# A two-layer trunk on one core: three adaLN vectors computed on TensorE, x loaded in two transfers, and a new order of the first part

## The chip, the cores and the metric

The kernel runs on 1 core of one Trainium2 chip. The metric is device time in microseconds of that core; several runs are given by their median.

## The reference

The input x has 512 tokens of 1024 channels, in float32. Two layers follow one another, and both get shift, scale and gate vectors from one conditioning vector c:

```python
c_act = jax.nn.silu(c)
for i in range(DEPTH):                        # DEPTH = 2
    mods = c_act @ w_ada[i] + b_ada[i]        # 6 vectors of 1024
    sh1, sc1, g1, sh2, sc2, g2 = split(mods, 6)
    h = rms_norm(x, norm1_g[i]) * (1 + sc1) + sh1
    mix = s5_mixer(h, ...) if i == 0 else short_conv_mixer(h, ...)
    x = x + g1 * mix
    h = rms_norm(x, norm2_g[i]) * (1 + sc2) + sh2
    x = x + g2 * swiglu(h, w_ffn_in[i], w_ffn_out[i])     # hidden size 2816
return rms_norm(x, final_g)
```

The S5 mixer runs a diagonal complex state space over 64 groups of 16 channels (64 states per group, discretised from a, b, c and a log step), then GELU and an output projection to 2048 columns whose halves are multiplied as value times sigmoid(gate) (the GLU).

## The kernel before, in words

The vectors of a layer are numbered m = 0 to 5 in the order shift 1, scale 1, gate 1, shift 2, scale 2, gate 2; (0, 2) is gate 1 of the first layer, (0, 4) and (0, 3) are scale and shift of its FFN.

The residual lives transposed in SBUF (`xT`, channels on partitions, 512 tokens along the free axis). Every large product is three products of float32r parts: `acc3` multiplies high by high, high by low and low by high. `Weights` streams weight blocks of 128x4x256 through three raw buffers (`wr`, 512 KB each, SP's queue, L158); ScalarE copies the high part `wh`, VectorE or GpSimd subtracts for the low part `wl`.

The first part (class `Ssm`, up to the GELU) is a set of coroutines: loads, constants, discretisation (`params`), matrices of a chunk of 8 tokens (`vb`, `vm`, `w1m`, `w3m`), a scan over 64 chunks (`sup`, `sdn`), outputs (`yi`, `ye`, `yt`). Their order is a table written out by hand, `ORDER`: a name stands for one step of that coroutine, `*n` for n steps, and a letter behind the name for the engine that does its copies (V is VectorE, A ScalarE, G GpSimd). Each engine issues in the order of the table, so a step that is moved there moves on every engine and queue that it uses. `pre` and `wprep` in the table are the first GLU products and the split of their weights.

SP's queue begins with `loads`: a (`nat`, L785 and L786), x in four transfers (`xtok`, L796), b (`xT` used as a scratch place, L799), and then the 16 blocks `aw` for shift and scale of the first norm (`aload`, L835). On x the first squares are taken by ScalarE (`squares`, L1097); on b the transposes `bps` and the discretised matrices depend.

The adaLN vectors come in two ways. Shift and scale of the first norm (`gemv`, `gvec`) are row products on TensorE: a column of c, broadcast to 32 weights, against 256 columns of w_ada, into one of four quadrants of 32 output rows (`gmv`), four products in a step. All the other ten vectors go through class `Ada`: a partition holds 32 input channels of 256 columns (`ada`, four transfers of 256 KB at a time), VectorE multiplies the first channel (L226) and multiplies and adds the other 31 (`aacc`, through the helper at L122), and two small products on TensorE with `nsel` (`adaps`) add up the partitions. `Ada.step(n)` does the next n channels. For the first three vectors these steps stand in ORDER (`adas`, with `adal` for the loads) or between the two last GLU halves; the rest stands in the two FFNs.

L124 is the helper of all matrix products, L125 of transposes, L116 of two-operand VectorE or GpSimd steps, L122 of the multiply-and-add, L123 of steps with scalars, L126 and L127 of copies on ScalarE and VectorE. In the page's names `o<-yT,wh` are GLU products, `yps` the products of the mixer's outputs, `sr` the chunk states that they read, `ssq` the sum of squares for the second norm, and `mod` an adaLN vector. The dense work after the GLU (FFN, convolution mixer, FFN, final norm) is in plain program order.

Of the kernel before, what the change touches and what calls it, by code (L numbers as in the profile page):

```python
# [34 lines left out]
loads aload squares.0*2 aload squares.0*2 aload consts aload*5 c_load aload params squares.1 params squares.1
aload squares.1 aload squares.1 aload params aload params*5 zero params zero params*10 zero params*69 b_in
cm44*2 b_in cm44 b_in cm44 b_in cm44 b_in cm44 b_in stats b_in*2 stats b_in*2 cm44 stats gemv.0 stats trans
stats*2 trans gemv.0 vb.0 trans vb.0 trans vm.0.0.2 vecs stats vecs gemv.0 stats vm.0.1.0.V gemv.0*2 trans vb.1
gemv.0 vb.1 vm.0.0.2 vm.1.1.3.G*3 aload*2 trans gemv.0 trans gemv.0 stats*2 vm.0.1.1.G trans vecs stats gvec.0
stats vm.0.1.3.V aload stats vm.0.1.3.V vm.0.1.1.G hrows.0.0 vm.0.1.1.G hrows.0.0 vm.0.1.3.V vm.0.1.0.V  # L40
vm.0.1.2.G hrows.0.0 vm.0.1.2.G hrows.1.0 vm.0.1.2.G hrows.0.0 gvec.0 c_in*4 gvec.0*2 vm.0.0.1 gvec.0
vm.0.0.0.G*2 hrows.0.1*2 vm.0.0.0.G gvec.0 vm.0.1.0.V hrows.0.1 gemv.1 hrows.0.1 vm.0.0.2 w1m.0.1.0*2 gemv.1
vm.0.0.1 rp.A.V gvec.0 rp.A.V w1m.0.1.2.V rp.A.V*3 gemv.1 rp.A.V*2 c_blocks rp.A.V vm.0.0.1 rp.A.V vm.0.0.3
rp.A.V w1m.0.1.2.V vm.0.0.3 rp.A.V vm.1.1.0.G rp.A.V w1m.0.0.0.V vm.1.1.0.G w1m.0.1.1.V vm.0.0.3 c_blocks
rows_t.0.0 gemv.1 rows_t.0.0 vm.1.1.0.G w1m.0.0.0.V w1m.0.1.1.V vm.1.1.2.G*3 w1m.0.0.3.V rows_t.0.1 gemv.1
rows_t.0.1 hrows.1.0 gemv.1 umod.0.0.VAVAVAVAVVVAVAVA*2 w3m.0.0.1*2 umod.0.0.VAVAVAVAVVVAVAVA w3m.0.0.1 gemv.1
w1m.0.0.3.V w1m.0.0.1.A umod.0.0.VAVAVAVAVVVAVAVA gemv.1 sm.0.0.A*2 umod.0.1.VAVAVAVAVAVAVVVV w1m.0.0.1.A
c_blocks dkm umod.0.1.VAVAVAVAVAVAVVVV sm.0.1.A w3m.0.1.1 umod.0.1.VAVAVAVAVAVAVVVV hrows.1.0 sm.0.0.A c_blocks
umod.0.1.VAVAVAVAVAVAVVVV sm.0.1.A vm.1.0.0.V*2 gvec.1*3 vm.1.0.0.V sm.0.1.A hrows.1.0 krev.0 w1m.0.0.2.A*2
w3m.0.1.1 w1m.0.1.3.A hrows.1.1 sup.0.0*4 hrows.1.1 sup.0.0 krev.0*2 sup.0.0*4 sm.0.2.A hrows.1.1 w3m.0.1.1  # L50
w1m.0.1.3.A sup.0.0*2 krev.0 kfin.0.S*4 w3m.0.0.0 kfin.0.S sup.0.0 gvec.1 w3m.0.0.0 sm.0.2.A w3m.0.0.0 sup.0.0
vm.1.0.3 sm.0.3.A vm.1.1.1.G vm.1.0.3*2 vm.1.1.1.G*2 sm.0.2.A w1m.1.1.2.A*2 sup.0.0 sm.0.3.A gvec.1 sm.0.3.A
kfin.0.S w1m.1.1.0.A sup.0.0 sup.0.1 sup.0.0 hrows.1.1 rows_t.1.0 sup.0.0 vm.1.0.2.G sup.0.0 kfin.0.S
w1m.1.1.3.A sup.0.1 sup.0.0 sup.0.1 rows_t.1.0 w1m.1.1.0.A sup.0.0*3 gvec.1 kfin.0.S*4 rows_t.1.1 sup.0.1
vm.1.0.2.G gvec.1 sup.0.1 sup.0.0 vm.1.0.2.G rows_t.1.1 w1m.1.1.3.A umod.1.0.VAVAAAVVAAAAVAAV sup.0.1 yi.0.2
sup.0.0 umod.1.0.VAVAAAVVAAAAVAAV*2 yi.0.2 sup.0.0*3 umod.1.1.VVAAAAVVVAVAVAAA w3m.0.1.0 sup.0.1 sup.0.0
w3m.0.1.0 umod.1.1.VVAAAAVVVAVAVAAA umod.1.0.VAVAAAVVAAAAVAAV w3m.0.1.0 sup.0.0 sup.0.1 sup.0.0
umod.1.1.VVAAAAVVVAVAVAAA*2 sup.0.1 vm.1.0.1.V*3 w3m.1.0.0 sdn.0.0 krev.1*2 w3m.1.0.0 krev.1*2 sup.0.1
w1m.1.1.1.A*2 sdn.0.0 sup.0.1 sdn.0.0 sup.0.1 sdn.0.0 w1m.1.0.3.A sup.0.1 wprep.0 sdn.0.0*2 adal sup.0.1*2
sdn.0.0 sup.0.1 w3m.1.0.0 w1m.1.0.1.A*2 sdn.0.0 w1m.1.0.0.A sup.0.1*2 sdn.0.0 sm.1.1.A w1m.1.0.3.A sm.1.1.A  # L60
sdn.0.0*2 yi.0.1 yi.0.0 w1m.1.0.2.A sup.0.1 wprep.0 sup.0.1*6 sm.1.1.A sup.0.1 w1m.1.0.0.A sdn.0.0 sw.0.0.AAAA
sup.0.1 yi.0.0 sw.0.0.AAAA sm.1.3.A sw.0.0.AAAA w3m.1.1.1*3 yi.0.1 sup.0.1 sw.0.0.AAAA ye.0.0*3 sup.0.1 ye.0.0
sm.1.3.A wprep.0 w1m.1.0.2.A sm.1.2.A yi.0.3 sm.1.3.A yi.0.3 ye.0.0 sm.1.2.A wprep.1 w3m.1.1.0 ye.0.0 w3m.1.1.0
adal sup.0.1 sdn.0.1*12 sw.0.1.VAAA*4 sm.1.0.A*3 w3m.1.1.0 adas.0*2 adal sm.1.2.A adas.0*3 ye.0.1 adas.0 adal
ye.0.1*2 x_t.0.0.A sup.1.0.G x_t.0.0.A*2 x_t.1.1.A ye.0.1*2 x_t.1.1.A sup.1.0.G*3 adal sup.1.1.P sup.1.0.G*3
x_t.1.0.A adas.0 kfin.1.B sup.1.0.G wprep.1 ye.0.1 sup.1.0.G x_t.0.0.A x_t.1.1.A sup.1.1.P yt.0.0*2 x_t.1.0.A
yt.0.0*4 kfin.1.B*2 sup.1.1.P yt.0.1 wprep.1 yt.0.1*3 x_t.1.1.A yt.0.1*2 sup.1.1.P*2 kfin.1.B sup.1.1.P*2 adas.0
sup.1.1.P*2 pre.0 wprep.2.G sup.1.1.P*3 wprep.2.G sup.1.1.P wprep.2.G sup.1.1.P sup.1.0.G kfin.1.B sup.1.0.G*3
wprep.3 kfin.1.B sup.1.0.G*3 x_t.1.0.A kfin.1.B*2 pre.0 kfin.1.B*2 sup.1.0.G*2 pre.0 sup.1.0.G kfin.1.B adas.0
# [1391 lines left out]
```

## Time and profile before

| what | value |
|---|---|
| median of 3 runs | 1192.04 us (1191.62 to 1195.54) |
| profiled execution | span 1196.1 us from its first to its last instruction; the page gives no other time for it |
| TensorE busy | 1104.6 us (92%), mean granted clock 0.968 |
| VectorE busy | 725.4 us (61%) |
| ScalarE busy | 389.7 us (33%) |
| GpSimd busy | 195.4 us (16%) |
| moved by DMA | 153.48 MB |

The page cuts the span in 40 slices of about 30 us. TensorE's row has 9 in nearly every slice from the tenth on, and lower digits in the first nine, while VectorE's row has its 8 and 9 in the first six slices. So the dense part is TensorE's, and the first 275 us have to be read by stages. A row of waits names the waiting engine and line, what released it, and then the total in us, the number of waits and the longest one. A row of the timeline gives start and duration, and in brackets the idle time before.

### The profile page before, as it was taken

Reading aid. Unit: us, or ns where it says so; the run is one execution under the profiler, and the core shown is the slowest. Engines: PE = TensorE matmul, PEld = TensorE weight load, DVE = VectorE, ACT = ScalarE, POOL = GpSimd, SP = SyncE. Lnnn points to the kernel's source line nnn. Section 1 sums busy time; section 2 is a strip of 40 time slices with the busy share of each in tenths; the row PEclk is TensorE's granted clock in tenths of the full one; section 3 lists DMA queues with packets and bytes.
Section 4 is the critical chain, followed back from the end, with each engine's and each line's share of the span. In section 5 each row is a group of like instructions: output and inputs, shape, how many; then the busy total and the mean of one; then the engine's idle time right before and its main releaser. Section 6 shows DMA issues by size and latency. Waiting matters only on the chain.

```text
span 1196.1 us, 15760 instructions
## 1 busy us (share of the span) xinstructions
PE 1104.6 (92%) x6146; PEld 932.3 (78%) x6146; DVE 725.4 (61%) x1334; ACT 389.7 (33%) x628; POOL 195.4 (16%) x141
## 2 busy tenths in 40 slices
...
GB/s 237 155 64 154 163 149 225 137 71 71 195 200 186 88 171 174 195 129 107 180 102 88 206 161 137 148 106 72 106 106 106 90 86 106 102 94 88 77 27 71
DMA packets 150107, 153.48 MB, mean 128 GB/s; under 512 B 8864, under 2 KB 144140, under 8 KB 150032
## 3 DMA queue, kind: packets, MB, share of 16 engines
...
q0 software_dynamic: 288, 0.10, 0.1%
...
HBM read 147.99 MB, written 2.10 MB: 125 GB/s over the span
## 4 chain that ended last, share of the span: by engine, by line
PE 76%; DVE 15%; DMA 3%; issue 2%; ACT 2%; POOL 2%; SPq 1%; DVEq 0%; ACTq 0%; POOLq 0%
PE o L124 71%; DVE aacc L122 4%; PE t L124 2%; DMA ada<-in_w_ada_dram 1%; DMA xT<-in_ssm_b_re_dram 1%; DVE sg L116 1%; DVE xT L122 1%; DVE sx L116 1%; DVE hlo L122 1%; POOL sx L116 1%; DMA wr<-in_ssm_w_out_dram 1%; DVE acc L116 1%; DVE v L116 1%; DVE wl L116 1%; DVE u L123 1%
## 5 line engine op out<-in xcount | busy, mean ns | idle before, releaser
L124 PE MATMUL o<-wide,wh 128*128 128x512 f32 (+1 forms) x992 | 364.5, 370 | 1.8 <-ACT wide L469 1.8
L124 PE MATMUL o<-wide,wl 128*128 128x512 f32 (+1 forms) x992 | 363.7, 369 | 0.0
L124 PE MATMUL o<-hlo,wh 128*128 128x512 f32 (+1 forms) x992 | 354.7, 370 | 2.3 <-DVE hlo L122 2.2
L126 ACT ACTIVATE wh<-wr 128x1024 fp32r<-128x1024 f32 (+1 forms) x184 | 188.5, 1039 | 416.9 <-PE o L124 294.0
L116 DVE TENSOR_TENSOR wl<-wr,wh 128x1024 fp32r<-128x1024 f32 (+1 forms) x155 | 185.0, 1204 | 156.9 <-ACT wh L126 155.1
L124 PEld LDWEIGHTS o<-wide,wh 128*128 128x128 f32 x992 | 187.9, 189 | 33.4 <-ACT wide L469 2.6
L124 PEld LDWEIGHTS o<-wide,wl 128*128 128x128 f32 x992 | 187.8, 189 | 30.9
L124 PEld LDWEIGHTS o<-hlo,wh 128*128 128x128 f32 x992 | 182.8, 189 | 34.7 <-DVE hlo L122 3.1
L124 PE MATMUL o<-hid,wh 128*128 128x512 f32 (+1 forms) x704 | 205.4, 375 | 0.0
L122 DVE SCALAR_TENSOR_TENSOR aacc<-ada,cper,aacc 128x256 f32<-128x256 f32 x310 | 187.4, 605 | 29.0 <-DMA ada<-in_w_ada_dram 20.5
L116 POOL TENSOR_TENSOR wl<-wr,wh 128x1024 fp32r<-128x1024 f32 x29 | 71.4, 2473 | 595.8 <-ACT wh L126 579.5
L124 PEld LDWEIGHTS o<-hid,wh 128*128 128x128 f32 x704 | 129.2, 188 | 23.7
L124 PE MATMUL o<-hid,wl 128*128 128x512 f32 (+1 forms) x352 | 131.8, 375 | 0.0
L116 DVE TENSOR_TENSOR sg<-sg,o 128x512 f32<-128x512 f32 (+1 forms) x50 | 31.7, 644 | 154.3 <-PE o L124 152.3
L124 PE MATMUL o<-yT,wh 128*128 128x512 f32 (+1 forms) x256 | 77.4, 383 | 13.8 <-DVE yT L116 10.1
L525 ACT ACTIVATE sg<-o 128x512 f32<-128x512 f32 (+1 forms) x48 | 26.8, 562 | 170.4 <-PE o L124 168.8
L124 PEld LDWEIGHTS o<-hid,wl 128*128 128x128 f32 x352 | 66.3, 188 | 11.9
L122 DVE SCALAR_TENSOR_TENSOR xT<-o,mod,xT 128x512 f32<-128x512 f32 (+1 forms) x56 | 38.8, 693 | 57.4 <-PE o L124 57.2
L124 PEld LDWEIGHTS o<-yT,wh 128*128 128x128 f32 x256 | 48.5, 198 | 23.4 <-issue 7.7
L124 PE MATMUL o<-yT,wl 128*128 128x512 f32 (+1 forms) x128 | 48.7, 380 | 0.0
L439 ACT ACTIVATE sq<-xT 128x256 f32<-128x256 f32 (+1 forms) x44 | 20.7, 472 | 62.9 <-DVE xT L122 57.3
L124 PE MATMUL o<-z,wh 128*128 128x512 f32 (+1 forms) x128 | 33.1, 348 | 4.6 <-ACT z L126 4.6
...
## 6 DMA issues: line engine op xcount, KB each, us to landing
wr<-in_w_ffn_in_dram SPq DMA_DIRECT2D x88, 512.0 KB, 3.6
...
wr<-in_w_ffn_out_dram SPq DMA_DIRECT2D x40, 512.0 KB, 4.4
wr<-in_conv_w_in_dram SPq DMA_DIRECT2D x24, 512.0 KB, 3.8
aw<-in_w_ada_dram SPq DMA_DIRECT2D x16, 512.0 KB, 10.2
wr<-in_ssm_w_out_dram SPq DMA_DIRECT2D x16, 512.0 KB, 9.1
wr<-in_conv_w_out_dram SPq DMA_DIRECT2D x8, 512.0 KB, 7.6
xtok<-in_x_dram SPq DMA_DIRECT2D x4, 512.0 KB, 8.2
```

The source lines that it names most:

```text
L116: (eng or e.V).tensor_tensor(out=out, in0=a, in1=b, op=op)
L122: e.stt = lambda o, a, s, b, op0, op1: e.V.scalar_tensor_tensor(out=o, in0=a, scalar=s, in1=b, op0=op0, op1=op1)
L123: e.ts = lambda o, a, s1, s2, op0, op1: e.V.tensor_scalar(out=o, in0=a, scalar1=s1, scalar2=s2, op0=op0, op1=op1)
L124: e.mm = lambda o, l, r, start, stop: e.PE.matmul(out=o, lhsT=l, rhs=r, start=start, stop=stop)
L126: e.cp = lambda o, i: e.A.activation(out=o, in_=i, func=AF.Copy)
L439: A.activation(out=q, in_=xT[:, k, SL[s]], func=AF.Square)
L525: A.activation(out=w, in_=g[:, 0:width(s)], func=AF.Silu)
```

## The change

It has four pieces.

1. (0, 2), (0, 4) and (0, 3) leave `Ada`, whose list now starts with (0, 5); `adal`, `adas` and the two `ada.step` calls of the GLU go. `gload` loads the columns of the three vectors as 12 blocks of 1 MB, and `gemm(m)` makes each vector by 32 row products on TensorE in four steps of eight, a copy by ScalarE, four small products with a new constant `sel2`, and an addition (for m = 4 a second VectorE step).
2. x comes in two transfers of 1 MB to 128 partitions instead of four of 512 KB to 64.
3. ORDER is a new table, with other steps side by side and other engines for some copies.
4. Comments are gone, so lines move by a few: the matrix helper is L120, two-operand steps are L112.

The diff, without comments and with one line of the table before and after:

```diff
+GEMV = (2, 4, 3)
 ORDER = """
-sup.1.0.G*3 pre.1 sup.1.0.G sup.1.1.P pre.1*6 sup.1.1.P adas.0 yi.1.0 sup.1.0.G sdn.1.1.G*5 sdn.1.0*5 yi.1.0
+sup.1.0.G sup.1.1.P gemm.4 sup.1.1.P pre.1*3 x_t.0.1 pre.1*2 yi.1.0 sup.1.0.G gemm.4 sup.1.0.G*7 sdn.1.0*4 yi.1.0
...
-    ada = e.ada = Ada(e, [(0, 2), (0, 4), (0, 3), (0, 5), (1, 1), (1, 0), (1, 2), (1, 4), (1, 3), (1, 5)])
+    ada = e.ada = Ada(e, [(0, 5), (1, 1), (1, 0), (1, 2), (1, 4), (1, 3), (1, 5)])
...
-        def adal():
-            for _ in range(8):
-                ada.load()
-                yield
-
-        def adas(v):
-            for _ in range(16):
-                ada.step(2)
-                yield
-            ada.finish()
-            yield
...
-            ssm.run(ORDER, dict(pre=pre, wprep=wprep, adas=adas, adal=adal))
+            ssm.run(ORDER, dict(pre=pre, wprep=wprep))
...
             glu(4 + q, tiles[q], tiles[2 + q], 0)
-        ada.step(12)
         tiles = half(1)
         for q in range(2):
             glu(q, tiles[q], tiles[2 + q], 0, (part[0][:, q], part[0][:, 2 + q]))
-        ada.step(20)
...
-        xs = a["x"][0].rearrange("(c j) d -> c j d", j=CH)
+        xs = a["x"][0].rearrange("(c j) (b n) -> b c j n", j=CH, n=256)
         for hf in range(2):
             self.xtok[hf] = self.small(f"xtok{hf}", [P, CH, 256])
-            for t in range(2):
-                b = hf * 2 + t
-                SP.dma_start(out=self.xtok[hf][t * 64:t * 64 + 64], in_=xs[:, :, b * 256:b * 256 + 256])
+            SP.dma_start(out=self.xtok[hf], in_=xs[2 * hf:2 * hf + 2])
...
+        self.sel2 = self.small("sel2", [P, 2])
+        e.add(self.sel2, idn[:, 0:P:64], idn[:, 32:P:64])
...
+    def gload(self):
+        e = self.e
+        for m in GEMV:
+            for z in range(2):
+                for kq in range(2):
+                    t = self.gt[(m, z, kq)] = e.big(f"gt{m}{z}{kq}").rearrange("p (k n) -> p k n", k=4)
+                    w = e.w_ada[0, kq * 512:kq * 512 + 512, m * D + z * 512:m * D + z * 512 + 512]
+                    e.SP.dma_start(out=t, in_=w.rearrange("(k p) n -> p k n", p=P))
+                    yield
+
+    def gemm(self, m):
+        e = self.e
+        ps = e.ps(f"gmm{m}")
+        for z in range(2):
+            for kq in range(2):
+                w = self.gt.pop((m, z, kq))
+                for ch in range(2):
+                    for kk in range(4):
+                        q = (2 * ch + kk % 2) * 32
+                        k = 4 * kq + kk
+                        e.mm(ps[q:q + 32, z * 256:z * 256 + 256], e.cvec[:, k:k + 1].to_broadcast([P, 32]),
+                             w[:, kk, ch * 256:ch * 256 + 256], k < 2, k > 5)
+                yield
+        ge = self.small("ge", [P, 512])
+        e.cp(ge, ps)
+        yield
+        pc = e.ps("gmc")
+        for b in range(4):
+            e.mm(pc[:, b * 2:b * 2 + 2], ge[:, b * P:b * P + P], self.sel2, True, True)
+        yield
+        v, b0 = e.mods[(0, m)], e.VB[(0, m)]
+        f = lambda t: t.rearrange("p (z c o) -> p z c o", z=2, c=2)
+        e.add(f(v), pc[:, 0:8].rearrange("p (z o c) -> p z c o", z=2, o=2), f(e.vec1[:, b0:b0 + KD]))
+        if m == 4:
+            e.stt(v, v, 1.0, e.vec1[:, e.VN2[0]:e.VN2[0] + KD], ALU.add, ALU.mult)
+        yield
```

The instructions stand as follows. First the head of SP's queue, before; `nat` is a, `xtok` x, `xT` b, `aw` the first block of w_ada.

```order
L785 DMA nat<-in_ssm_a_re_dram 64x64
L786 DMA nat<-in_ssm_a_im_dram 64x64
L796 DMA xtok_101<-in_x_dram 64x8x256 x2
L796 DMA xtok_104<-in_x_dram 64x8x256 x2
L799 DMA xT<-in_ssm_b_re_dram 16x2x1024 x2
L799 DMA xT<-in_ssm_b_im_dram 16x2x1024 x2
L835 DMA aw_130<-in_w_ada_dram 128x2x512
```

The same place of SP's queue after the change.

```order
L767 DMA nat<-in_ssm_a_re_dram 64x64
L768 DMA nat<-in_ssm_a_im_dram 64x64
L776 DMA xtok_101<-in_x_dram 128x8x256
L776 DMA xtok_103<-in_x_dram 128x8x256
L779 DMA xT<-in_ssm_b_re_dram 16x2x1024 x2
L779 DMA xT<-in_ssm_b_im_dram 16x2x1024 x2
L815 DMA aw_128<-in_w_ada_dram 128x2x512
```

Nothing changes its place; each half of x is one transfer to 128 partitions, whose source runs over two column blocks, 64 chunks, 8 tokens and 256 columns in this order, and b still stands behind x.

Next VectorE at the end of the second half of the mixer, before: `sr` copies chunk states, `wl` splits a weight block, `aacc` is the adaLN sum, `yT` the mixer's output.

```order
L127 COPY sr_1729<-sx_1122 64x512 x2
L116 TENSOR_TENSOR wl_1738<-wr_1573,wh_1737 128x1024
L116 TENSOR_TENSOR wl_1745<-wr_1742,wh_1744 128x1024
L116 TENSOR_TENSOR mod_78<-adaps_1748,vec_75 128x2x4
L226 TENSOR_SCALAR aacc<-ada_1369,cper 128x256
L122 SCALAR_TENSOR_TENSOR aacc<-ada_1369,cper,aacc 128x256 x5
L116 TENSOR_TENSOR wl_1767<-wr_1764,wh_1766 128x1024
L122 SCALAR_TENSOR_TENSOR aacc<-ada_1369,cper,aacc 128x256 x2
L127 COPY sr_1729<-sx_1122 64x512 x3
L122 SCALAR_TENSOR_TENSOR aacc<-ada_1797,cper,aacc 128x256
L632 MEMSET cv 128x2 x2
L122 SCALAR_TENSOR_TENSOR aacc<-ada_1797,cper,aacc 128x256 x7
```

VectorE at the same place after it.

```order
L112 TENSOR_TENSOR mod_80<-gmc,vec_75 128x8
L118 SCALAR_TENSOR_TENSOR mod_80<-mod_80,vec_75 128x8
L112 TENSOR_TENSOR scq<-sx_1110,cop 128x480
L112 TENSOR_TENSOR sx_1110<-sx_1110,scq 128x15x16 x2
L123 COPY sr_1788<-sx_1110 64x512 x3
L112 TENSOR_TENSOR wl_1744<-wr_1650,wh_1743 128x1024
L112 TENSOR_TENSOR wl_1808<-wr_1652,wh_1807 128x1024
L112 TENSOR_TENSOR wl_1812<-wr_1790,wh_1811 128x1024
L123 COPY sr_1788<-sx_1110 64x512 x3
L112 TENSOR_TENSOR wl_1880<-wr_1792,wh_1879 128x1024
L112 TENSOR_TENSOR yT_1873<-ytp,yT_1872 128x2x256 x3
L112 TENSOR_TENSOR mod_79<-gmc,vec_75 128x8
```

The sums `aacc` between the copies and splits are gone; of the vectors only their last additions (`mod`) are left.

Last TensorE around the first GLU product (`o<-yT,wh`), before: `xtp` transposes x, `ytp` the mixer's output, `krt` is a kernel matrix of the second half.

```order
L125 MATMUL xtp<-ident,xtok_104 128x128 x8
L125 MATMUL ytp<-ident,yt 128x128 x8
L124 MATMUL krt<-dk,ident 128x512
L124 MATMUL krt<-ident,ks 128x128 x4
L125 MATMUL ytp<-ident,yt 128x128 x8
L124 MATMUL o_1453<-yT_1402,wh_1160 128x512
```

TensorE there after the change, with `gmm` the row products and `gmc` the small ones.

```order
L121 MATMUL xtp<-ident,xtok_101 128x128 x4
L120 MATMUL gmm_1297<-gt_1246,cvec 32x256 x8
L120 MATMUL gmm_1297<-gt_1290,cvec 32x256 x8
L121 MATMUL xtp<-ident,xtok_101 128x128 x4
L121 MATMUL xtp<-ident,xtok_103 128x128 x4
L120 MATMUL gmc<-sel_153,ge 128x2 x4
L121 MATMUL ytp<-ident,yt 128x128 x12
L120 MATMUL krt<-dk,ident 128x512
L120 MATMUL krt<-ident,ks 128x128 x4
L120 MATMUL gmm_1461<-gt_1428,cvec 32x256 x8
L121 MATMUL ytp<-ident,yt 128x128 x4
L121 MATMUL xtp<-ident,xtok_103 128x128 x4
```

Three of the twelve steps of row products stand here ahead of the first GLU product, two stand earlier among the products of the mixer, and the other seven stand among the GLU products and the second half of the mixer.

More of the change, by code (lines that the diff above doesn't have):

```diff
@@ L33 @@
 PAIRS = D // 256
+GEMV = (2, 4, 3)
 ORDER = """
[L35 to L69, printed above, removed]
@@ L70 @@
-wprep.3 sup.1.1.P*3 adas.0 x_t.1.0.A sup.1.1.P x_t.0.1 pre.0 sup.1.1.P wprep.3 sup.1.1.P x_t.0.1 sup.1.1.P*2
-adas.0*2 pre.0 wprep.4.V x_t.0.1 pre.0*2 adas.0 sup.1.0.G*2 sup.1.1.P*6 sup.1.0.G*4 pre.0 adas.0 x_t.0.1
-sup.1.0.G*3 pre.1 sup.1.0.G sup.1.1.P pre.1*6 sup.1.1.P adas.0 yi.1.0 sup.1.0.G sdn.1.1.G*5 sdn.1.0*5 yi.1.0
-sdn.1.0*3 yi.1.1 sdn.1.1.G*2 yi.1.1 sdn.1.1.G*5 pre.1 adas.0 w3m.1.0.1 yi.1.2*2 w3m.1.0.1 sdn.1.0*4
-sw.1.0.VVAA*2 yi.1.3 wprep.4.V*2 w3m.1.0.1 wprep.5.V*3 adas.0 adas.1*3 yi.1.3 sw.1.0.VVAA*2 wprep.6.V*3 adas.1
@@ L75 @@
-ye.1.0 wprep.7.G sw.1.1.VVAV ye.1.0*5 sw.1.1.VVAV*3 adal adas.1*2 adal*2 adas.1 wprep.7.G*2 adas.1*2 pre.3*2
-yt.1.0 pre.3 yt.1.0 adas.1 ye.1.1*6 yt.1.0 pre.3*2 adas.1*2 yt.1.0*2 adas.1*4 pre.3*2 yt.1.0 pre.3 pre.2*4
-yt.1.1 adas.1 yt.1.1*5
+loads aload squares.0*2 aload squares.0*2 aload consts aload*5 c_load aload params squares.1 params squares.1 aload
+squares.1 aload squares.1 aload params aload*2 params*2 zero params*8 zero params*68 b_in params*4 stats params*3
+b_in*4 stats*2 b_in*3 cm44*6 stats trans*2 b_in gemv.0*2 cm44 vb.1 vb.0 trans stats*2 trans*2 stats vm.1.1.3.G vecs*2
@@ new lines @@
+b_in vm.1.1.3.G vm.0.0.2 gemv.0 vb.1 stats*3 vm.0.0.2 vm.1.1.3.G vm.0.1.1.G*3 trans*2 vecs gemv.0*3 aload gemv.0*2
+vm.0.1.2.G stats gvec.0 stats*2 gvec.0*2 zero hrows.0.0*2 trans aload hrows.0.0 vm.0.1.3.V*2 gvec.0 vm.0.1.0.V
+hrows.1.0*2 vm.0.1.2.G c_in vm.0.1.3.V vm.0.1.0.V vm.0.0.1 vm.0.1.2.G vm.0.0.0.G vb.0 gvec.0 vm.0.0.0.G*2 c_in*2
+hrows.0.1 gemv.1 c_in hrows.0.1*2 vm.0.1.0.V w1m.0.1.0*2 hrows.0.0 vm.0.0.1 gvec.0 vm.0.0.1 vm.1.1.0.G w1m.0.0.1.A
+gemv.1*4 gvec.0 gemv.1 rp.A.V*2 c_blocks w1m.0.1.2.V w1m.0.1.1.A gemv.1 rp.A.V*4 vm.0.0.3*2 rp.A.V*5 w1m.0.0.0.V*2
@@ new lines @@
+vm.0.0.3 w1m.0.0.3.A hrows.0.1 hrows.1.0 vm.0.0.2 w1m.0.1.2.V rows_t.0.0*2 rows_t.0.1*2 c_blocks w1m.0.1.1.A
+w1m.0.0.3.A vm.1.1.0.G*2 rp.A.V vm.1.1.2.G*3 w3m.0.0.1*3 umod.0.0.VAVAVAVAVVVAVAVA*4 gemv.1 sm.0.0.A*2
+umod.0.1.VAVAVAVAVAAAVVVV*3 c_blocks w1m.0.0.1.A sm.0.1.A dkm hrows.1.1 umod.0.1.VAVAVAVAVAAAVVVV c_blocks sm.0.0.A
+hrows.1.1 sm.0.1.A krev.0 vm.1.0.0.V gvec.1 sm.0.1.A sup.0.0*3 w1m.0.1.3.A*2 w1m.0.0.2.A*2 krev.0*3 kfin.0.S*3
+vm.1.0.0.V hrows.1.0 sup.0.0 vm.1.0.0.V sup.0.0 gvec.1 sup.0.0*2 w3m.0.1.1 sup.0.0 sm.0.3.A sup.0.0 hrows.1.1
@@ new lines @@
+sup.0.0*2 sm.0.2.A w3m.0.1.1 sup.0.0 vm.1.0.3 kfin.0.S*2 sm.0.2.A gvec.1*2 w3m.0.1.1 sup.0.0 w3m.0.0.0 sm.0.2.A
+w3m.0.0.0*2 w1m.1.1.2.A*2 vm.1.1.1.G*2 vm.1.0.3 sup.0.0*2 sm.0.3.A vm.1.0.3 sm.0.3.A sup.0.0 kfin.0.S gvec.1 sup.0.0
+sup.0.1*2 sup.0.0*2 w1m.1.1.3.A*2 sup.0.1 sup.0.0 hrows.1.1 sup.0.0 rows_t.1.0*2 vm.1.1.1.G sup.0.1 w1m.1.1.0.A
+vm.1.0.2.G gvec.1 w1m.1.1.0.A vm.1.0.2.G*2 sup.0.0 gvec.1 sup.0.1 sup.0.0 umod.1.0.VAVAAAVVAAAAVAAV sup.0.0
+rows_t.1.1*2 sup.0.1 kfin.0.S*5 yi.0.2*2 sup.0.0 umod.1.0.VAVAAAVVAAAAVAAV*2 sup.0.0 umod.1.1.VVAAAAVVVAVAVAAA
@@ new lines @@
+w3m.0.1.0*3 sup.0.1*2 sup.0.0*2 umod.1.1.VVAAAAVVVAVAVAAA w1m.1.1.1.A sup.0.0*2 gload umod.1.0.VAVAAAVVAAAAVAAV
+umod.1.1.VVAAAAVVVAVAVAAA*2 vm.1.0.1.V*2 sup.0.1 w1m.1.1.1.A vm.1.0.1.V w1m.1.0.1.A sdn.0.0 krev.1 w1m.1.0.1.A
+w3m.1.0.0*3 sup.0.1 krev.1 wprep.0 sdn.0.0 krev.1 sup.0.1 sdn.0.0*2 sup.0.1*2 wprep.1 sup.0.1 w1m.1.0.0.A sup.0.1*2
+w1m.1.0.3.A sdn.0.0 sup.0.1*2 sdn.0.0 sm.1.1.A krev.1 sm.1.1.A wprep.0 sdn.0.0*3 yi.0.0 sup.0.1 sdn.0.0 sup.0.1
+sdn.0.0*2 sup.0.1 w1m.1.0.0.A yi.0.0 sup.0.1*2 w1m.1.0.3.A sm.1.3.A sm.1.1.A w1m.1.0.2.A sw.0.0.AAAA*4 w3m.1.1.1
@@ new lines @@
+yi.0.1*2 w1m.1.0.2.A ye.0.0*2 sup.0.1*5 yi.0.3 ye.0.0 sup.0.1 sm.1.3.A sm.1.2.V gload wprep.0 sup.0.1 sm.1.3.A
+sm.1.2.V gload w3m.1.1.1 sdn.0.1*2 w3m.1.1.1 sdn.0.1 sm.1.0.A sdn.0.1*5 w3m.1.1.0*3 sm.1.0.A*2 yi.0.3 ye.0.0 sdn.0.1
+gload sdn.0.1*3 sw.0.1.VAAA*2 gemm.2*2 sw.0.1.VAAA*2 sup.1.0.G sm.1.2.V ye.0.1*3 x_t.1.1.A ye.0.0 sup.1.0.G*4 ye.0.0
+sup.1.0.G*3 ye.0.1*2 sup.1.1.P*3 x_t.1.1.A x_t.1.0.V x_t.0.0.V gemm.2 sup.1.1.P kfin.1.B sup.1.1.P gemm.2 x_t.0.0.V*2
+sup.1.1.P*3 gemm.2 wprep.1 ye.0.1 x_t.1.1.A gemm.2 sup.1.1.P*3 yt.0.0 x_t.1.0.V sup.1.1.P*2 gload*2 sup.1.1.P yt.0.0
```

11 lines of the change are left out of this document (10 added, 1 removed).

## The prediction

> **What bounds the kernel now.** I read the time by stages first: where each engine is full. The columns are the busy times of TensorE, its weight loads, VectorE, ScalarE and GpSimd, then the granted TensorE clock, the DMA share and GB/s.
>
> ```profile
> 0.00:20.00 20.00, 3.29 (x32) 3.08 (x33) 16.28 (x96) 9.48 (x34) 10.96 (x18) 1.00 0.93 167
> 20.00:40.00 20.00, 10.48 (x92) 5.77 (x93) 18.07 (x38) 7.31 (x29) 13.52 (x14) 0.87 1.03 333
> 22.00:103.00 81.00, 57.91 (x794) 40.06 (x794) 77.48 (x201) 46.04 (x114) 68.74 (x45) 0.83 0.46 138
> 103.00:222.60 119.60, 95.89 (x545) 78.86 (x540) 108.66 (x163) 42.17 (x63) 67.18 (x58) 0.90 0.83 180
> 222.60:275.40 52.80, 42.07 (x304) 41.52 (x302) 44.55 (x98) 22.10 (x43) 19.12 (x9) 0.84 0.23 70
> 275.40:1196.10 920.70, 903.48 (x4468) 767.11 (x4468) 478.12 (x781) 268.38 (x374) 29.42 (x12) 1.00 0.49 123
> ```
>
> Behind 275.4 us TensorE is busy 903.48 of 920.70 us, so nothing that the change does before gives more there than a shift of the start. From 22 to 103 us VectorE is full (77.48 of 81 us). From 103 to 222.6 us VectorE (108.66) and TensorE (95.89 of 119.6) limit each other. The next two views say how: VectorE's sums for the adaLN vectors in that stretch, then TensorE's waits between 103 and 260 us.
>
> ```profile
> 103.00:222.60 119.60, 1.11 (x8) 1.05 (x8) 82.08 (x96) 0.90 0.83 180
> ```
>
> ```profile
> PE o L124 <- DVE yT L116: 10.1, 2, 7.2
> PE yps L124 <- DVE sr L127: 9.2, 2, 8.4
> PE ssq L124 <- DVE acc L116: 6.1, 1, 6.1
> PE o L124 <- DVE mod L116: 3.7, 1, 3.7
> ```
>
> The 96 steps of three vectors take 82.08 of VectorE's 108.66 us, and TensorE waits 23.0 us there for VectorE's `yT`, `sr` and `mod`.
>
> Last the start: the chain of waits up to 22 us, the head of ScalarE's timeline, and how long transfers of SP's queue take from issue to landing (x's are given as shortest, median and longest).
>
> ```profile
> 2.01 0.59 SPq L796
> ...
> 4.72 0.70 SPq L799
> 5.42 0.04 issue
> 5.46 12.14 DMA xT<-in_ssm_b_re_dram
> 17.60 0.14 issue
> 17.74 1.94 PE bps L125 x16
> ```
>
> ```profile
> 9.80 1.28 ACT L1097 ACT_TABLE_LOAD   x1 [9.80 <-DMA xtok<-in_x_dram]
> ```
>
> ```profile
> DMA to landing us min/median/max: 5.0/8.2/11.5
> ```
>
> Everything starts when b lands at 17.60 us. b stands behind x on SP's queue, and ScalarE too has nothing to do until x is there at 9.80.
>
> **The three vectors.** The 96 steps go (82.08 us of VectorE). What can be won is TensorE's waiting behind them.
>
> - The waits on `yT`, `sr` and `mod`, 10.1 + 9.2 + 3.7 = 23.0 us, lose what VectorE was doing. If they all go, −23.0. What is late next is the scan: `sr` copies states that GpSimd helps to make, and GpSimd is busy 67.18 of 119.6 us, so a part may come back; I take −23.0 with 0 to 8 given back in the range.
> - TensorE runs slowly behind such gaps. These are two runs of the same 32 products, one behind 0.84 us of idle time and one behind 8.36:
>
> ```profile
> 150.30 2.25 PE L124 MATMUL yps<-w,sr 128*64 128x128 f32 x32 [0.84 <-DVE sr L127]
> 169.84 4.12 PE L124 MATMUL yps<-w,sr 128*64 128x128 f32 x32 [8.36 <-DVE sr L127]
> ```
>
> The stage's clock of 0.90 costs some 95.89 × 0.10 = 9.6 us. Half of it goes with the two longest gaps (estimate): −4.8. [...]
>
> - `ssq` waits 6.1 us for the squares at the end of the GLU. The 32 sums that stood between the halves of the GLU in VectorE's order are no longer ahead of them, but its own GLU steps are: half, −3.0 (0 to −6.1).
> - `adaps` (1.11 us of TensorE) goes and the `gmc` products come: 0. The `mod` additions stay.
> - Between 22 and 103 us two of four copies `xT<-w1p` move from VectorE to ScalarE:
>
> ```profile
> L127 DVE COPY xT<-w1p 128x512 f32<-128x512 f32 x4 | 2.6, 683 | 0.0
> ```
>
> 2 × 0.683 = −1.4 on the full engine. The copies that go the other way lie in the stretch where VectorE is freed: 0, and if it weren't freed, their sum of a few times 0.7. GpSimd's wide memset, moved behind the matrices, is hidden here by the wait for b up to 17.60: 0.
>
> Against this, TensorE gets 12 steps of eight products. The nearest rows are the steps of four products for the first norm, here with what starts behind them:
>
> ```profile
> 46.18 1.08 PE L124 MATMUL gmv<-aw,cvec 128*32 128x256 f32 x8
> 47.19 1.12 PE L125 MATMUL w1p<-ident,v 128*128 128x128 f32 x4
> ...
> 53.01 0.64 PE L124 MATMUL gmv<-aw,cvec 128*32 128x256 f32 x8
> 53.58 0.46 PE L125 MATMUL up<-ident,hrow 64*128 64x64 f32 x8
> ```
>
> Four products (eight records) hold TensorE for 0.57 us at full clock and 1.01 at the low one. In these steps each product goes into another quadrant. In `gemm` the quadrants alternate between two only, four products long. If the four quadrants overlapped fully before and now two do, a step of eight takes 4 × 0.57 = 2.28 us; if nothing is lost, 2 × 0.57 = 1.14. No row decides; I take the middle, 1.7: 12 × 1.7 = +20.4 (13.7 to 27.4). All of it is on the path as soon as TensorE no longer waits.
>
> The bytes loaded are the same (3 × 4 MB), in 12 transfers for 48. But `gload` stands in SP's queue between weight blocks, whose issues wait for the splits:
>
> ```profile
> SPq L158 <- POOL wl L116: 47.9, 10, 13.4
> ```
>
> A block of w_ada behind such a wait comes late, and a `gemm` step inline on TensorE then holds up all products behind it. Ten waits, 4.8 us each; the loads are mostly issued some steps ahead: +1.5 (0 to 6).
>
> Sum: −23.0 − 4.8 − 3.0 − 1.4 + 20.4 + 1.5 = −10.3, with ends near −25 and 0. So the work that leaves VectorE comes back on TensorE for the most part.
>
> **x in two transfers.** The bytes and the run length (1 KB) are the same. What changes is the outer loop. Before, a transfer had 64 partitions on the one side and 512 rows of tokens on the other. Now the target has 128 partitions, and the source begins with a loop of 2 (column blocks), and only then come the 512 rows. The other transfers of the queue's head have 16 or more on both sides (b 16, a 64, `aw` 128), so no row of this trace shows how a transfer is handed to the 16 DMA engines when one side begins with 2. The two ends:
>
> - All 16 engines, as before: 0 us (fewer issues, some −1).
> - Two engines, if the work is cut only along an outer loop that both sides share (128 and 2 have 2 in common). Then each carries 1 MB of x's 2 MB. What one engine moves comes from these rows: a weight block's and a's landing, and the DMA share from 8 to 10 us.
>
> ```profile
> wr<-in_w_ffn_in_dram SPq DMA_DIRECT2D x88, 512.0 KB, 3.6
> ...
> nat<-in_ssm_a_re_dram SPq DMA_DIRECT2D x1, 16.0 KB, 2.0
> ```
>
> ```profile
> 8.00:10.00 2.00, 0.00 (x0) 0.00 (x0) 2.00 (x3) 0.20 (x1) 2.00 (x2) 1.00 1.15 204
> ```
>
> A block of 512 KB in runs of 1 KB, with nearly nothing else under way, takes 3.6 − 2.0 = 1.6 us beyond a small one: 32 KB per engine, 20.5 GB/s. The 20 to 40 us row gives 333/1.03/16 = 20.2. x itself in the crowded start had 204/16 = 12.8. So 1.05 MB on one engine takes 51, 52 or 82 us. I take 51, since two engines alone are nearest to the uncrowded row. b's share on those two engines stands behind it (32 KB each, 1.6 us): b lands at 2.0 + 2.0 + 51 + 1.6 = 56.6 instead of 17.6, a shift of +39. Upper end +70. The lower end is 24 GB/s (a fifth above the row, estimate), +31. What hides it? The chain above starts with b, VectorE and ScalarE issue in order, so next to nothing: VectorE's 16.28 us before are those steps that need neither x nor b.
>
> I take two engines. [...]
>
> [...]
>
> **The sum.** The profiled execution spans 1196.1 us, 0.3% above the median of 1192.04; I set the differences against the median: 1192.0 + 39 − 10.3 = 1220.7, so 1220. Its own range: −25 to 0 for the vectors and +31 to +70 for x, the ends not met together: 1204 to 1250.
>
> **The rivals.**
> - A, on the other side: x is spread over all 16 engines. Place: x's landing, 9.80 us for ScalarE. Then 1192.0 − 10.3 = 1182 (1167 to 1192). For it: every transfer in this trace does so, the DMA share being 0.93 in the first 20 us. Against it: none of them begins with a loop of 2. It decides as soon as x lands before some 20 us.
> - B: x is on two engines, but b isn't held up by all of it, for instance because b's pieces go on while x's last are under way and the first work needs half of x only. Then the shift is half of it, about 20: 1192 + 20 − 10.3 = 1202 (1195 to 1210). Against it: b landed 12.14 us behind its issue, as a queue does.
> - C: x is spread, but the row products eat the gain: 27.4 for them, 6 for late blocks, and 5 of the 23 come back: 1192 − 32.2 + 33.4 + 5 = 1198, and with half of these 1190, within 0.3% of before. For it: GpSimd's share and the waits of SP. Against it: VectorE is busy only 26.6 us of this stretch without the sums.
>
> **How the numbers follow.** Forecast (two engines) 0.65, A 0.20, B 0.10, C 0.05. A measurement of this kernel tells about 0.3% (3.6 us) from no change. Faster takes A without its upper tail and a little of C: 0.21. Same: the tail of A and most of C: 0.06. Slower: forecast and B, 0.73. The range leaves out the lower part of A below 1178 and the tail above 1247: 1178 to 1247. The likeliest one's own range is 1204 to 1250.
>
> **What the profile after would show.** Right: x's longest landing some 50 us; a low DMA share (some 2/16) with about 40 GB/s from 10 to 50 us; the first `bps` near 57; the steps up to the first GLU product later by about as much, then the stretch from it to the FFN shorter by some 10 us, no wait on `yT` or `sr` above 3 us, a `gmm` step near 1.7 us. Wrong: x landed by 15 us, which gives A; `gmm` steps at 1.14 or 2.28, which moves the sum by 7; TensorE waiting for `gt` transfers or for states from GpSimd. The forecast would be wrong altogether if DMA engines share a transfer without regard to its loops, or if one engine alone moves far more than 20 GB/s.

## The result

| kernel | median of the runs | against the kernel before |
|---|---|---|
| before | 1193.79 us (1191.62 to 1196.54, 4 runs) | |
| changed | 1206.09 us (1204.09 to 1208.58, 4 runs) | 1.0115, 95% interval 1.0094 to 1.0137 |

The changed kernel is 12.3 us slower. The forecast was 1220 within 1178 to 1247, slower by 28 against the median known then, so the direction is right and the size is less than half of it. The profiled execution spans 1202.3 us; that of before spans 1196.1.

The changed kernel's start, in stretches of 10 us with the columns of the prediction (10 to 20, 30 to 40, 40 to 50 and 50 to 60 us):

```profile
10.00:20.00 10.00, 0.00 (x0) 0.00 (x0) 4.54 (x42) 0.00 (x0) 0.00 (x0) 1.00 0.14 47
...
30.00:40.00 10.00, 0.00 (x0) 0.00 (x0) 0.00 (x0) 2.10 (x9) 0.00 (x0) 1.00 0.14 46
40.00:50.00 10.00, 0.00 (x0) 0.00 (x0) 0.00 (x0) 0.00 (x0) 0.00 (x0) 1.00 0.52 94
50.00:60.00 10.00, 2.81 (x26) 2.81 (x26) 0.00 (x0) 3.41 (x14) 0.00 (x0) 1.00 0.90 213
```

DMA moves 46 GB/s at a share of 0.14 of 16 engines, that is 2.2 of them, until about 45 us; the 20 to 40 us of before moved 333. The compute engines have next to nothing to do. The tile of x says who waits for it, and TensorE's waits add b:

```profile
  ACT junk L1080: 47.8, 2
  DVE s L112: 46.1, 1
```

```profile
PE bps L121 <- DMA xT<-in_ssm_b_re_dram: 52.7, 1, 52.7
```

The slow transfers hold SP's queue as well. These are the issues of x before and after the change (shortest, median and longest in ns, then the first and the last start in us), and then, all after the change, the DMA share in tenths in 40 slices of 1.5 us up to 60 us, the start of the squares of x's second half, and b's last two transfers (the last number is the time from issue to landing in us):

```profile
L796 SPq DMA_DIRECT2D xtok<-in_x_dram x4: 592/627/679, 2.0 to 4.0; - x4
...
L776 SPq DMA_DIRECT2D xtok<-in_x_dram x2: 635/10118/19602, 2.0 to 2.7; - x2
...
DMA  0123211111111111111111111111115999999479
...
56.40 0.52 ACT junk L1080 x2
...
xT<-in_ssm_b_im_dram SPq DMA_DIRECT2D x2, 128.0 KB, 11.7
```

Issuing the second half of x took 19.6 us, where each quarter took 0.6 before. b's first issue, at 22.3 us, then took 22.8, and its other three follow from 45.1 to 46.1. From there on the DMA engines are busy (a share of 0.90 from 50 to 60 us), and x's second half and b land 11 to 12 us later, at 56.4 and 57.2.

Where the time stands further on is read best from four marks on TensorE: the first transposes of b (`bps`), the first GLU product (`o<-yT,wh`), the first product of the GLU's last part, the second half of the tokens (`t<-yT,wh`), and the first low-part product of the FFN (`o<-hlo,wh`). These are the rows of their tiles; behind the durations stand the first and the last start. Before:

```profile
L125 PE MATMUL bps<-ident,xT x32: 283/292/294, 17.7 to 21.4; 32*128 32x32 f32 x32
L124 PE MATMUL o<-yT,wh x256: 277/389/796, 120.0 to 233.2; 128*128 128x512 f32 x96, 128*128 128x256 f32 x32
L124 PE MATMUL t<-yT,wh x64: 279/283/582, 233.3 to 259.9; 128*128 128x256 f32 x64
L124 PE MATMUL o<-hlo,wh x992: 274/389/415, 261.8 to 1148.3; 128*128 128x512 f32 x162, 128*128 128x256 f32 x37
```

Changed:

```profile
L121 PE MATMUL bps<-ident,xT x32: 289/292/313, 57.2 to 60.6; 32*128 32x32 f32 x32
L120 PE MATMUL o<-yT,wh x256: 278/389/504, 152.5 to 253.0; 128*128 128x512 f32 x96, 128*128 128x256 f32 x32
L120 PE MATMUL t<-yT,wh x64: 279/283/581, 253.2 to 271.6; 128*128 128x256 f32 x64
L120 PE MATMUL o<-hlo,wh x992: 274/389/415, 273.6 to 1153.7; 128*128 128x512 f32 x162, 128*128 128x256 f32 x37
```

The start is later by 39.5 us; up to the FFN 27.7 of them are won back (7.0, 12.6 and 8.1 us in the three stages), and at the FFN 11.8 are left, close to the 12.3 between the medians. Behind that mark the two profiles differ by another 5.6 us (934.3 against 928.7), which belongs to the executions and not to the kernels. 4.4 of it are a wait for the convolution's `z`, before and then after:

```profile
PE o L124 <- ACT z L126: 4.6, 1, 4.6
```

```profile
PE o L120 <- ACT z L122: 0.2, 1, 0.2
```

In the ten profiles of this study this wait lies between nothing and 4.6 us, and the stretch behind the mark between 928 and 934 us with it, whichever the kernel. So the comparison below goes by medians and by the three stages ahead of the mark.

### The profile page after: what moved, and what is told of

Same layout as the page of the kernel before. It is cut to its first block, busy times and chain, and to the rows that moved or that the text cites. A ratio compares the mean times of both kernels' runs of the same rounds, so it can differ in the third digit from the quotient of the medians.

```text
span 1202.3 us, 16010 instructions
## 1 busy us (share of the span) xinstructions
PE 1105.4 (92%) x6350; PEld 932.7 (78%) x6350; DVE 643.3 (54%) x1243; ACT 389.1 (32%) x628; POOL 188.4 (16%) x140
## 4 chain that ended last, share of the span: by engine, by line
PE 76%; DVE 11%; DMA 5%; ACT 4%; another core or an unknown queue 2%; issue 1%; SPq 0%; DVEq 0%; ACTq 0%
PE o L120 71%; DMA xtok<-in_x_dram 2%; DMA ada<-in_w_ada_dram 2%; PE t L120 2%; DVE sx L112 1%; DVE scq L112 1%; DVE sg L112 1%; DVE aacc L118 1%; DMA wr<-in_ssm_w_out_dram 1%; DVE xT L118 1%; DVE hlo L118 1%; DVE wl L112 1%; DVE acc L112 1%; ACT junk L1080 1%
## 5 line engine op out<-in xcount | busy, mean ns | idle before, releaser
L120 PE MATMUL o<-wide,wh 128*128 128x512 f32 (+1 forms) x992 | 364.3, 370 | 1.8 <-ACT wide L453 1.8
L120 PE MATMUL o<-wide,wl 128*128 128x512 f32 (+1 forms) x992 | 363.4, 369 | 0.0
L120 PE MATMUL o<-hlo,wh 128*128 128x512 f32 (+1 forms) x992 | 354.7, 370 | 2.3 <-DVE hlo L118 2.2
L112 DVE TENSOR_TENSOR wl<-wr,wh 128x1024 fp32r<-128x1024 f32 (+1 forms) x156 | 186.2, 1205 | 162.8 <-ACT wh L122 161.1
L120 PEld LDWEIGHTS o<-wide,wh 128*128 128x128 f32 x992 | 187.6, 189 | 33.3 <-ACT wide L453 2.6
L120 PEld LDWEIGHTS o<-wide,wl 128*128 128x128 f32 x992 | 187.6, 189 | 31.2
L120 PEld LDWEIGHTS o<-hlo,wh 128*128 128x128 f32 x992 | 182.8, 189 | 34.5 <-DVE hlo L118 3.1
L120 PE MATMUL o<-hid,wh 128*128 128x512 f32 (+1 forms) x704 | 205.3, 375 | 0.0
L112 POOL TENSOR_TENSOR wl<-wr,wh 128x1024 fp32r<-128x1024 f32 x28 | 69.4, 2491 | 571.6 <-ACT wh L122 548.7
L120 PEld LDWEIGHTS o<-hid,wh 128*128 128x128 f32 x704 | 129.2, 188 | 23.7
L120 PE MATMUL o<-hid,wl 128*128 128x512 f32 (+1 forms) x352 | 131.8, 375 | 0.0
L112 DVE TENSOR_TENSOR sg<-sg,o 128x512 f32<-128x512 f32 (+1 forms) x50 | 31.7, 644 | 177.2 <-PE o L120 152.3
L118 DVE SCALAR_TENSOR_TENSOR aacc<-ada,cper,aacc 128x256 f32<-128x256 f32 x217 | 108.3, 499 | 17.6 <-DMA ada<-in_w_ada_dram 11.6
L120 PEld LDWEIGHTS o<-hid,wl 128*128 128x128 f32 x352 | 66.3, 188 | 12.0
L120 PE MATMUL o<-yT,wh 128*128 128x512 f32 (+1 forms) x256 | 72.6, 366 | 0.0
L118 DVE SCALAR_TENSOR_TENSOR xT<-o,mod,xT 128x512 f32<-128x512 f32 (+1 forms) x56 | 38.8, 693 | 57.2 <-PE o L120 57.0
L120 PEld LDWEIGHTS o<-yT,wh 128*128 128x128 f32 x256 | 46.1, 189 | 8.2 <-issue 0.4
L121 PE MATMUL bps<-ident,xT 32*128 32x32 f32 x32 | 3.7, 293 | 52.7 <-DMA xT<-in_ssm_b_re_dram 52.7
L120 PE MATMUL o<-yT,wl 128*128 128x512 f32 (+1 forms) x128 | 46.5, 363 | 0.0
L121 PEld LDWEIGHTS bps<-ident,xT 32*128 32x128 f32 x32 | 3.6, 198 | 52.8 <-DMA xT<-in_ssm_b_re_dram 52.8
```

Source lines behind the costliest of these rows:

```text
L112: (eng or e.V).tensor_tensor(out=out, in0=a, in1=b, op=op)
L118: e.stt = lambda o, a, s, b, op0, op1: e.V.scalar_tensor_tensor(out=o, in0=a, scalar=s, in1=b, op0=op0, op1=op1)
L120: e.mm = lambda o, l, r, start, stop: e.PE.matmul(out=o, lhsT=l, rhs=r, start=start, stop=stop)
L121: e.tr = lambda o, i, idn: e.PE.transpose(out=o, in_=i, identity=idn)
```

## The experiments

**The changed kernel with x in four transfers.** x's loads of before, all else as changed.

```diff
-        xs = a["x"][0].rearrange("(c j) (b n) -> b c j n", j=CH, n=256)
+        xs = a["x"][0].rearrange("(c j) d -> c j d", j=CH)
...
-            SP.dma_start(out=self.xtok[hf], in_=xs[2 * hf:2 * hf + 2])
+            for t in range(2):
+                b = hf * 2 + t
+                SP.dma_start(out=self.xtok[hf][t * 64:t * 64 + 64], in_=xs[:, :, b * 256:b * 256 + 256])
```

> The changed kernel with x again in four transfers of 64 partitions, nothing else undone. Theory (x's two transfers, whose source begins with a loop of 2, run on two DMA engines and hold up the whole start): the first transposes of b start near 18 us as before instead of 57.2, and the time falls by the 39.5 us of that shift, from 1206.1 to about 1167 (1162 to 1172), so faster than before by some 27 us. Rival 1 (x's late landing is partly hidden, and the new order of the steps costs time elsewhere): it falls by 15 to 25 only, to 1181 to 1191. Rival 2 (the transfers are not the cause): 1206.

Measured: 1168.87 us, 0.9797 of before (0.9772 to 0.9823), 37.2 us less than the changed kernel. Its marks:

```profile
L121 PE MATMUL bps<-ident,xT x32: 282/292/294, 17.7 to 21.3; 32*128 32x32 f32 x32
L120 PE MATMUL o<-yT,wh x256: 277/389/504, 113.2 to 212.3; 128*128 128x512 f32 x96, 128*128 128x256 f32 x32
L120 PE MATMUL t<-yT,wh x64: 278/283/420, 212.4 to 230.1; 128*128 128x256 f32 x64
L120 PE MATMUL o<-hlo,wh x992: 274/389/415, 232.0 to 1115.3; 128*128 128x512 f32 x162, 128*128 128x256 f32 x37
```

The start is back at 17.7 us, and the stages behind it take what they took in the changed kernel (95.5, 99.2 and 19.6 against 95.3, 100.7 and 20.4). x's transfers cost their shift and little else, and the other two pieces win 24.0 us. This version beats both kernels.

**The kernel before with x in two transfers.** The same edit the other way round.

> The kernel before with x in two transfers, nothing else changed. Theory (the shift does not depend on the order of the steps, since VectorE and ScalarE issue in order and all work behind the start needs x or b): the first transposes of b at about 57 us and 1194 + 39 = 1233 (1228 to 1238). Rival (the order of the steps before hides a part, since its first VectorE steps need only b and its squares come before the constants): 1215 to 1228.

Measured: 1233.01 us, 1.0339 (1.0303 to 1.0375), +40.2.

```profile
L125 PE MATMUL bps<-ident,xT x32: 290/292/314, 57.4 to 60.9; 32*128 32x32 f32 x32
```

The shift has the same size in both orders, so the order of before hides none of it.

**The changed kernel with x in four transfers that keep the loop of 2.** Each half of x is cut by columns.

```diff
-            SP.dma_start(out=self.xtok[hf], in_=xs[2 * hf:2 * hf + 2])
+            for z in range(2):
+                h = slice(128 * z, 128 * z + 128)
+                SP.dma_start(out=self.xtok[hf][:, :, h], in_=xs[2 * hf:2 * hf + 2, :, :, h])
```

> The changed kernel with x in four transfers that all still begin with the loop of 2 on the source's side: each half of x is cut by columns into two transfers of 512 KB with runs of 512 bytes. Theory (the outer loop of 2 confines a transfer to two engines, whatever its size and number): DMA moves no more than 46 GB/s until x is there, the transposes of b start at 57 us or later (up to 100 if a run of 512 bytes takes as long as one of 1 KB), and the time is 1206 or more. Rival (the size of 1 MB or 128 target partitions make it slow): as with four transfers, 1169 to 1175.

Measured: 1215.73 us in one run. From 10 to 50 us every stretch reads like this one (TensorE alone is shown ahead of clock, share and GB/s), and the transposes start at 62.5:

```profile
20.00:30.00 10.00, 0.00 (x0) 1.00 0.15 40
```

```profile
L121 PE MATMUL bps<-ident,xT x32: 284/292/294, 62.5 to 65.9; 32*128 32x32 f32 x32
```

Number and size of the transfers are as in the fast version, and it is slow all the same. Its runs of 512 bytes are no reason either, since the changed kernel is slow with runs of 1 KB, as the fast version has them. The size of 1 MB isn't it: the changed kernel's blocks of w_ada have 1 MB and land in a median of 7.3 us, and their outer loops are 128 on both sides.

```profile
gt<-in_w_ada_dram SPq DMA_DIRECT2D x12, 1024.0 KB, 7.3
```

What is common to the slow transfers is the loop of 2 at the outside of the source.

**The changed kernel with b ahead of x.** b's four `dma_start` lines stand ahead of x's two.

> The changed kernel with b's four transfers issued ahead of x's two; x still in two transfers. It tells apart which late arrival decides. Theory (x itself decides: VectorE's statistics stand ahead of b's steps and need ScalarE's squares of x): transposes of b start below 15 us, but VectorE still waits until about 60 us, and the time is 1206 within 4 us. Rival (b, queued behind x on two engines, decides): about 1170 to 1180.

Measured: 1209.90 us, 1.0135 (1.0101 to 1.0169), within 4 us of the changed kernel. The transposes of b, and VectorE's wait:

```profile
L121 PE MATMUL bps<-ident,xT x32: 288/292/294, 7.1 to 10.5; 32*128 32x32 f32 x32
```

```profile
DVE s L112 <- ACT junk L1080: 47.7, 1, 47.7
```

b is there 50 us earlier and nothing is won: VectorE stands in its first statistics step, which needs the squares of x. So x itself holds up the start. Whether a late b alone would do so too was not tried.

**The kernel before with the row products alone.** The three vectors as in the change, in the table of before: loads where `adal` stood, a step of products where the fourth part of a vector's sums was done. One line of the table:

```diff
-adal sup.0.1 sdn.0.1*12 sw.0.1.VAAA*4 sm.1.0.A*3 w3m.1.1.0 adas.0*2 adal sm.1.2.A adas.0*3 ye.0.1 adas.0 adal
+gload sup.0.1 sdn.0.1*12 sw.0.1.VAAA*4 sm.1.0.A*3 w3m.1.1.0 gload sm.1.2.A gemm.2 ye.0.1 gload ...
```

> The kernel before with only the three vectors moved to the row products: a step of eight products stands where the last sum of its block stood, the loads where the loads stood, and gate 1's, scale 2's and shift 2's last steps at the end of the second half; x in four transfers and the order of the rest as before. The prediction's sum gave -10.3 us for the vectors (-25 to 0) with 1.7 us for a step. With the 0.95 us that a step takes in the changed kernel's trace it gives -19. Theory (the vectors carry most of the gain of some 27 us): 1168 to 1178. Rival (the new order carries most of it): 1180 to 1190. That the loads now come late where nothing was laid out anew could hold it at 1194.

Measured: 1181.69 us, 0.9902 (0.9875 to 0.9929), −11.2 against the before of the same comparison (1192.85). In its trace one load comes late:

```profile
PE gmm L124 <- DMA gt<-in_w_ada_dram: 6.0, 1, 6.0
```

The waits on `yT` and `mod` are gone, and that for VectorE's `sr` is down to 1.1 us. The time lies in the range of the rival: the new order, worth some 13 us more, is as large as the vectors.

**The same with one load earlier.** The sixth load of w_ada moves ahead of weight block 4 (`wprep.4`), whose issue waits for a free buffer.

```diff
-... sup.1.1.P*2 gemm.2 pre.0 wprep.4.V x_t.0.1 pre.0*2 ... sw.1.1.VVAV*3 gload*3 ...
+... sup.1.1.P*2 gemm.2 pre.0 gload wprep.4.V x_t.0.1 pre.0*2 ... sw.1.1.VVAV*3 gload*2 ...
```

> The kernel before with the three vectors as row products, and the sixth load of w_ada moved ahead of the fourth weight block on SP's queue; nothing else differs from the run with the vectors alone, which took 1181.7 us and in whose trace one step of products waits 5.97 us for that load. Theory (what the new table gives beyond the vectors is, next to loads that come in time, work laid out better): the wait of 6.0 goes with some 2 us of slow clock behind it, 1173 to 1176, and 4 to 7 us to the changed kernel with four transfers (1168.9) remain. Rival 1 (late loads are all of it): 1169. Rival 2 (the wait is replaced by another): 1180 to 1182.

Measured: 1177.68 us, 0.9875 (0.9839 to 0.9910). The wait of 6.0 us is gone, and the stage from the first GLU product to `t` is down from 112.2 to 107.2 us; a wait of 3.1 us for the copy behind the products is new, and the end of the GLU is 1.4 us longer (24.2 against 22.8). The median falls by 4.0, less than the 5.7 to 8.7 expected. Some 9 us to the new order remain. Three rows tell where: the stage between the first GLU product and `t`, first in this kernel, then in the changed one with four transfers; and this one's wait at the end of the GLU.

```profile
115.00:222.20 107.20, 104.08 (x729) 83.78 (x726) 39.08 (x79) 40.42 (x58) 58.26 (x53) 0.98 0.55 175
```

```profile
113.20:212.40 99.20, 98.72 (x667) 81.00 (x666) 39.47 (x71) 38.77 (x56) 60.32 (x56) 1.00 0.55 167
```

```profile
PE ssq L124 <- DVE acc L116: 3.0, 1, 3.0
```

With the new order TensorE is busy nearly without a gap in that stage (98.72 of 99.2) at full clock. Five of the twelve steps of products lie ahead of the first GLU product, where this kernel has two; that is 2.8 us of work, in a stage that doesn't get longer by it (95.5 against 97.6). The end of the GLU is 4.6 us shorter (19.6 against 24.2), and the wait at it is down to 0.7 us.

**The order of the products in a step.** The changed kernel with four transfers, but two products for one quadrant follow one another.

```diff
-                    for kk in range(4):
+                    for kk in (0, 2, 1, 3):
                         q = (2 * ch + kk % 2) * 32
```

> The changed kernel with four transfers of x, and the eight products of a step in another order: two products for the same quadrant behind one another, then the next quadrant. In the changed kernel they alternate between two quadrants, and a step takes 0.95 to 1.02 us, as if all four overlapped. The prediction's 1.7 us rested on products overlapping only with their neighbours in other quadrants. If neighbours decide, a step takes 1.7 to 2.3 us here and the kernel some 9 to 15 us more; if only the amount of work in each quadrant counts, 0.95 to 1.1 us and the time stays at 1169 within 4 us.

Measured: 1166.12 us in one run. A double and a single step of the changed kernel, each with what starts behind it, and then the same two places here:

```profile
163.60 1.96 PE L120 MATMUL gmm<-gt,cvec 128*32 128x256 f32 x32
165.49 1.09 PE L121 MATMUL xtp<-ident,xtok 128*128 128x128 f32 x8
...
182.04 1.08 PE L120 MATMUL gmm<-gt,cvec 128*32 128x256 f32 x16
183.06 1.97 PE L120 MATMUL yps<-wide,u 128*64 128x128 f32 x32
```

```profile
125.69 1.97 PE L120 MATMUL gmm<-gt,cvec 128*32 128x256 f32 x32
127.59 1.09 PE L121 MATMUL xtp<-ident,xtok 128*128 128x128 f32 x8
...
144.16 1.09 PE L120 MATMUL gmm<-gt,cvec 128*32 128x256 f32 x16
145.18 1.97 PE L120 MATMUL yps<-wide,u 128*64 128x128 f32 x32
```

Two steps take 1.89 and 1.90 us, one takes 1.02 in both. Which quadrant the neighbour writes makes no difference here.

**b ahead of x, with x in four transfers, and VectorE's first statistics step behind b's first steps.** It was to fill 5.53 us in which VectorE stands idle.

```diff
-b_in params*4 stats params*3 b_in*4 stats*2 b_in*3 cm44*6 stats trans*2
+b_in params*7 b_in*7 stats*3 cm44*6 stats trans*2
```

> A version to beat both: the changed kernel with x in four transfers, b's transfers ahead of x's, and VectorE's first statistics step behind b's first steps. In the run with four transfers VectorE stands idle for 5.53 us at 14.6 us, waiting for ScalarE's squares of x. Theory (VectorE is full from there to the first GLU product, so what it does in that gap is won): 2 to 5 us, 1164 to 1167. Rival (x lands some 2.5 us later behind b, and the chain from the squares through the statistics to the rows decides): 1169 to 1172.

Measured: 1171.45 us, 0.9814 (0.9789 to 0.9839), not better than without it. The transposes start at 8.5, but VectorE's wait for the squares grows:

```profile
DVE s L112 <- ACT junk L1082: 8.4, 1, 8.4
```

x lands later behind b, so the rival holds: the chain through x and its squares decides at the start here too.

## Why the prediction was right or wrong

**x in two transfers: right in mechanism, as far as share and rate tell; that the size came out so well is partly luck.** Forecast were 51 us on two engines, b at 56.6 us and a shift of 39. Measured are 46 GB/s, b's transposes at 57.2, a shift of 39.5, and 37.2 and 40.2 us for the same edit in two kernels. Behind this stand two terms that were off in opposite ways. If two engines did the work, one moved 23 GB/s (half of 46), not the 20.5 of the uncrowded block, so x's 2.1 MB take 45.6 us at this rate instead of 51 (an estimate; the slow stretch ends at about 45). And b did not land 1.6 us behind x. Three of its four issues came only at 45.1 to 46.1 us, since SP itself was held up, and they took 11.7 to 12.0 us to land among the loads issued behind them, about as long as before (12.1). Why x's second half, too, landed only at 56.4 us the profile does not show. A share of 0.14 is 2.2 of 16 engines: that two engines did the work is inferred from the share and the rate, since the rows do not name the engines. That a transfer is cut along a loop that both of its sides share was the author's assumption, and no run shows it; the 51 us on two engines and the shift of 39 rest on it. What the runs show is a share of 0.14 with 46 GB/s in the changed kernel, of 0.15 with 40 GB/s in the version of four transfers that keeps the loop of 2, and 37.2 us less with x's loads of before.

**What stands behind x: half right.** The prediction let everything start with b. With b early the time did not fall, since VectorE's first statistics step waits for x itself. Rival B, which let b go ahead, has no gain to give for that reason.

**The three vectors: the sum came out, but two of its terms were wrong in opposite ways.** −10.3 were forecast, and −11.2 measured with nothing else changed. The row products were put at 20.4 us, 1.7 a step. The steps of the changed kernel, four double ones at 1.89 and four single ones at 1.02, make 11.6; in the run with the vectors alone they make 12.8, with one step of 1.88 right behind the late load. The mistake was the middle between a full overlap of four quadrants and one of two, both of them estimates. Even the lower end, 1.14, was too high, since it doubled a step of four products: 4, 8 and 16 products take 0.57, 1.02 and 1.89 us, so a second step right behind the first costs 0.87. Late loads were put at 1.5 us, and with the table of before a single one cost 6.0 (the bound of the range). With 12.8 and 6.0 in their places, and without the −1.4 for copies, which belongs to the new table, the sum is −12.0. So the other terms fit as a whole, and the agreement of −10.3 is partly luck. The waits on `yT` and `mod` went altogether, `sr` nearly so, and `ssq` went from 6.1 to 3.0 as forecast. TensorE's idle time up to the FFN fell from 56.5 to 37.8 us. Its busy time rose by 7.3 only, with 12.8 us of products new, at a faster clock (0.97 for 0.91 from the first GLU product to `t`).

**The new table: the step that failed.** The prediction costed it by the engines to which copies move, −1.4 us, and took the rest of the order as neutral. It is worth 12.8 us against the table of before with the same products (1168.87 against 1181.69), of which 4.0 go to one load in time. The sum for vectors and table, −10.3, was −24.0, at the end of the range given for it (−25 to 0). So the changed kernel lies at the low end of the forecast's own range (1204 to 1250), and the forecast of 1220 was 14 us too slow. The direction held because x's shift is larger than even this gain. The profile of before had hints: the order only counts where engines wait, and the rows of waits and of clock told how much waiting there was, but nothing of which row a new order removes. The order of the changed kernel showed five of the twelve steps ahead of the first GLU product; the prediction priced all twelve on the path.

**Rivals A and C** fell with x's landing: x was not spread over all engines (a share of 0.14), and the row products did not eat the gain.

Left open: which moves of the table make the remaining 9 us. The stages tell where they lie (2.1, 8.0 and 4.6 us in the three stages of the two profiles; behind the FFN's mark the faster kernel's execution gives 3.4 us back, 2.6 of them in the wait for `z`), but no move was tried by itself.
